# One core, hybrid MLA and mLSTM backbone: an early constant load, six banks for the output-gate tiles, a first chunk in stream tiles, and the values' products ahead of the convolution

## The chip, the cores and the metric

The kernel runs on one core of a Trainium2 chip. The metric is the device time of that core in microseconds (us), as the median of several runs; lower is better. Beside the runs there is one profiled execution with a trace of every instruction, and the profile is a view of that trace. PE is the matrix engine, PEld its weight loads, DVE, ACT and POOL the vector, scalar and general engines, SP the engine that issues the DMAs (SPq is its queue).

## The reference

Two layers run over 1024 latent tokens and 256 context tokens of width 1024. Layer 0 is multi-head latent attention. Layer 1, where the change lies, is a bidirectional mLSTM with 8 heads of 256 columns (16 blocks of 128, called features here). Cut to what matters:

```python
xm, z, og = jnp.split(h @ w_in, 3, axis=-1)
xc = jax.nn.silu(centred_dwconv(xm, conv_w, conv_b))      # 5 taps along the tokens
q, k, v = blockdiag(xc, w_q), blockdiag(xc, w_k), blockdiag(xm, w_v)
qkv = jnp.concatenate([q, k, v], axis=-1)
g = qkv @ w_if + b_if                                     # per direction: input and forget gate of 8 heads
li, lf = g[..., :8], jax.nn.log_sigmoid(g[..., 8:])
# per head and direction, chunk by chunk:
C_new = decay * C + einsum('bhl,bhld,bhle->bhde', a_end, vv, kk)   # running-max stabilised
hh    = num / maximum(abs(den), exp(-m))
y = ((rmsnorm(sigmoid(og) * h) * head_norm + skip * xc) * silu(z)) @ w_out
```

The kernel computes all of it in float32; each large product is three passes over a high and a low part (wh, wl for weights, hT..h, hT..l for tokens).

## The kernel before, in words

Layer 1 runs as stages, one after the other.

**Convolution stage** (phase_a, L911 to L1036). One turn of its loop per feature f. PE makes the columns xm of the *next* feature (tiles xps, by L78 to L80), the folded key-query matrix G and the gate columns gw of this one (pf, L980 to L982), the gate sums of all features in three banks (gps, L1011), the values (L1024, copied by ACT to vt at L1025 and stored to v_d) and the queries (qt, L1032). DVE does the four later taps (L995). At the end ACT copies the gate sums to graw (L1036).

**Gate scan** (gate_scan, L1210), a generator whose steps are taken inside the next stage. It loads a selection matrix sel and a bias (L1222, L1224), multiplies graw with sel (gsel, L1236), takes log-sigmoid and the running sums and maxima on DVE (gb, gM, gR), and turns the results by 40 PE transposes (gT, L1293) into column form (gcol, L1295). Tile gT has one bank, gsel two.

**Output-gate stage** (phase_z, L1093). For 8 heads, 2 halves of the contraction and 4 token tiles it runs 64 groups of 12 matmuls of 128x256 (po), in an order of PE and ACT that is written by hand. POOL splits the weights of w_og (wh, wl); ACT takes the sigmoid out of PSUM (og, L1136), SP stores it to og_d. Tiles po have five banks. The scan's steps stand before groups 0, 2, 32 and 37; before groups 39, 45, 51 and 57 the class Quarters prepares the next stage (L1080 on DVE, high parts t0h to t3h on ACT, low parts on DVE).

**Branch gate** (branch_gate, L1142): y products, PE without a pause.

**Recurrence** (phase_b, L1300). Chunks of 256 tokens. states() at L1357 loads x and v of a chunk from DRAM, transposes x on PE (S, L1369), splits the result (thh, thl) and forms the state updates pc and C. Before it, og0() issues the loads and splits of head 0's share of w_og for the remaining token tiles (L1047); the products of those tiles are dealt between the chunks by gate().

For engines other than PE and ACT in the output-gate stage, a scheduler sets the order from the order of the code. The lists of DMAs on SP and the lists of each engine run strictly in order. W.raw() and W.pair() hand out stream tiles from a small ring: a new load waits until the tile's earlier user is done.

Of the kernel before, what the change touches and what calls it, by code (L numbers as in the profile page):

```python
# [11 lines left out]
F32 = mybir.dt.float32  # L12
# [4 lines left out]
PSUM = bass.MemoryType.PSUM  # L17
# [895 lines left out]
def phase_a(nc, tc, ops, A, consts, mod, hT, S, W, graw, wx0, late):  # L913
# [3 lines left out]
    with ExitStack() as es:  # L917
# [49 lines left out]
        for f in range(NF):  # L967
# [21 lines left out]
                ops.split(g4[:, x, :, :8], g4[:, x, :, 8:16], pv, "act", "dve")  # L989
            xm = [sp.tile([P, CONV_W], F32R, name=f"xm{i}", bufs=1) for i in "hl"]  # L990
            ops.split(xm[0], xm[1], xp[:, 2 : 2 + CONV_W], "pool", "dve")
            xc = sp.tile([P, CONV_W], F32, name="xc")
            nc.scalar.activation(xc, xp[:, :CONV_W], AF.Identity, scale=cw[:, f, 0:1], bias=cw[:, f, 5:6])  # L993
            for j in range(1, 5):
# [13 lines left out]
            for b, (c0, n) in enumerate(cols):  # L1008
                for x, op in ((1, xm), (0, xh)):
                    for i in range(2):  # L1010
# [4 lines left out]
                            start=f == 0 and x == 1 and i == 0,  # L1015
                            stop=f == NF - 1 and x == 0 and i == 1,
                        )

            vt = sp.tile([P, NT, P], F32, name="vt")
            for t0, n in ((0, 2), (2, 4), (6, 4)):  # L1020
                ps = pm.tile([P, 4, P], F32, name="m")
                for i in range(n):
                    c0 = (t0 + i) * P + (4 if t0 else 2)
                    nc.tensor.matmul(ps[:, i], xp[:, c0 : c0 + P], bv, start=True, stop=True)  # L1024
                nc.scalar.copy(vt[:, t0 : t0 + n], ps[:, :n])  # L1025
            nc.sync.dma_start(S["v"][:, f * P : (f + 1) * P].rearrange("(c p) d -> p c d", p=P), vt)

            qt = qp.tile([P, SEQ], F32, name="qt")
            for j in range(2):
# [66 lines left out]
def phase_z(nc, tc, ops, A, hT, S, W, tiles, scan, e1, es):  # L1096
# [3 lines left out]
        tc.tile_pool(name=name, bufs=bufs, reuse_waits="tile", side="right", **kw)  # L1100
    )
    with ExitStack() as ez:
        sp, pp = right(ez, "z_s", 4), right(ez, "z_p", 5, space=PSUM)

        steps = {0, 2, 32, 37}
        later = (39, 45, 51, 57)
# [104 lines left out]
def gate_scan(nc, tc, ops, A, consts, S, keep, raw, es):  # L1211
# [6 lines left out]
    dec = keep.tile([P, 2, MH, NCH], F32, name="decay")  # L1218
    pl = lambda name, bufs=1, **kw: es.enter_context(tc.tile_pool(name=name, bufs=bufs, reuse_waits="tile", **kw))
    sp, pp = pl("g_s"), pl("g_p", 1, space=PSUM)  # L1220
    sel = sp.tile([P, 2, GR], F32, name="sel")
    nc.sync.dma_start(sel, A["gate_sel"])  # L1222
    bias = sp.tile([GR, 2], F32, name="gbias")
    nc.sync.dma_start(bias, A["b_if"])  # L1224
    keep01 = sp.tile([GR, T], F32, name="keep01")
    nc.sync.dma_start(keep01, A["chunk_keep"])
    yield
# [58 lines left out]
    yield  # L1286
    for c0 in range(0, NT, 3):
        n = min(3, NT - c0)
        pt = pp.tile([P, 3, 4, GR], F32, name="gT")
        for i in range(n):  # L1290
            for q in range(4):
                src = R[:, q] if q < 3 else gg
                nc.tensor.transpose(pt[:, i, q], src[:, (c0 + i) * P : (c0 + i + 1) * P], consts["idn"][:GR, :GR])  # L1293
        for d, r in enumerate(rows):
            nc.vector.tensor_copy(cols[d][:, c0 : c0 + n], pt[:, :n, :, r.start : r.start + MH])  # L1295
# [4 lines left out]
def phase_b(nc, tc, ops, A, consts, S, W, cols, dec, hT, es_h, es_w):  # L1300
# [3 lines left out]
    with ExitStack() as es, ExitStack() as ew, ExitStack() as eo:  # L1304
# [51 lines left out]
        def states(h, step, st):  # L1356

            for c in news[step]:
                hd = slice(h * 256, (h + 1) * 256)
                x = st["x"][c] = xp.tile([P, 2, U], F32, name="x", bufs=8)  # L1360
                nc.sync.dma_start(x, S["xcT"][2 * h : 2 * h + 2, :, c * U : (c + 1) * U].rearrange("k p t -> p k t"))
                v = st["v"][c] = vp.tile([P, 2, VW], F32, name="v", bufs=7)
                nc.sync.dma_start(v[:, :, :256], S["v"][c * U : (c + 1) * U, hd].rearrange("(a p) d -> p a d", p=P))
                nc.gpsimd.memset(v[:, :, 256:257], 1.0)
                nc.gpsimd.memset(v[:, :, 257:258], 0.0)
                pt = pw.tile([P, 2, 2, P], F32, name="S")
                for a in range(2):
                    for k in range(2):
                        nc.tensor.transpose(pt[:, a, k], x[:, k, a * P : (a + 1) * P], consts["idn"])  # L1369
                th = st["th"][c] = [sp.tile([P, 2, 256], F32R, name=f"th{i}", bufs=THB) for i in "hl"]  # L1370
                ops.split(th[0], th[1], pt.rearrange("p a k f -> p a (k f)"), "act", "dve")
            for i in (2 * step, 2 * step + 1):
                for d in range(2):
                    update(h, d, i, st)

            for d in range(2):
                if step == 1:
                    update(h, d, NCH - 2, st)
                if step == 3:
                    t, nxt = ORDERS[d][-2:]  # L1380
                    decay(h, d, t, st, st["C", d, nxt][0])
# [104 lines left out]
        new = lambda: {"x": {}, "v": {}, "th": {}}  # L1486
        ogs = lambda h: output_gate(nc, ops, A, S, hT, (W, po), h, range(NZ, 8))
        og0, *ogt = ogs(0)
        og0()
        o = W.raw().rearrange("p (t n) -> p t n", t=8 - NZ)  # L1490
        sts = [new() for _ in range(MH)]
        for step in range(NU - 1):
            states(0, step, sts[0])
            gate(0, ogt[step], o)
        units = [(h, c, sts[h]) for h in range(MH) for c in range(1, NU)]
        front(*units[0])
# [137 lines left out]
def build(nc, tc, A, out, dbg=None):  # L1634
    ops = Ops(nc)
    with ExitStack() as es:
# [30 lines left out]
        with ExitStack() as el:  # L1667
# [15 lines left out]
                el2.close()  # L1683

            gr = el.enter_context(tc.tile_pool(name="graw", bufs=1))
            graw = gr.tile([P, T], F32, name="graw")
            phase_a(nc, tc, ops, A, consts, mod, hT, S, W, graw, wx0, late)
            with ExitStack() as e1:
                scan = gate_scan(nc, tc, ops, A, consts, S, gk, graw, e1)
                next(scan)  # L1690
                with ExitStack() as et:
                    (cols, dec), Q = phase_z(nc, tc, ops, A, hT, S, W, range(NZ), scan, e1, et)
                    branch_gate(nc, tc, ops, A, S, W, Q)
# [106 lines left out]
```

## Time and profile before

| what | value |
|---|---|
| median of 3 runs | 2325.61 us (2319.2, 2325.61, 2329.93) |
| profiled execution | 2333.05 us |
| span of its trace, mean granted PE clock | 2331.3 us, 0.983 |
| PE, DVE, ACT, POOL busy | 95%, 72%, 53%, 51% |
| convolution stage, most of it | 1180 to 1410 us, PE busy 228.94 of 230 |
| its end and the output-gate stage | 1409 to 1527 us |
| branch gate to recurrence | 1655 to 1700 us, PE busy 36.87 of 45 |

PE is busy 95% of the span, so what it still loses lies in few places. A share over the whole span hides them; they are found by the waits of PE in a stretch, by the chain of waits, and by a table of stretches with the granted clock.

### The profile page before, as it was taken

The numbers are of one execution on the slowest core, as the hardware profiler recorded it, in microseconds if no ns is written. First come the engines' busy times: TensorE is split into PE (matmuls) and PEld (weight loads), VectorE is DVE, ScalarE is ACT, GpSimd is POOL, SyncE is SP. The second block draws the span as 40 slices with busy tenths as digits, with TensorE's granted clock in tenths as the row PEclk, the third lists the DMA queues.
The fourth block names the chain that finished last, engine by engine and source line by source line (L and its number), as shares of the span: only waits on it lengthen the run. The fifth ranks groups of instructions, "written<-read, shape, count | busy, mean of one in ns | idle before, by whom it ended". The sixth has DMA issues, their size and how long they took to land.

```text
span 2331.3 us, 38227 instructions
## 1 busy us (share of the span) xinstructions
PE 2216.7 (95%) x13404; PEld 1945.4 (83%) x13404; DVE 1670.8 (72%) x2871; ACT 1235.7 (53%) x2937; POOL 1186.6 (51%) x1586
## 2 busy tenths in 40 slices
PE   8999999999999999998999999899899999998998
PEld 4877798998998988887888887888788888896787
DVE  5588598999998988457765556554398888888321
ACT  4612487787887877332333333343466766676211
POOL 3324356565655645463332235622457778878321
PEclk9999999999999999999999999999999999999999
DMA  7066522222311211643444433423635555545531
GB/s 263 28 213 221 153 71 79 69 63 68 89 45 59 82 54 45 198 152 125 136 165 136 136 111 97 133 101 109 203 108 157 164 163 165 165 140 168 181 127 54
DMA packets 191579, 291.11 MB, mean 125 GB/s; under 512 B 14392, under 2 KB 134968, under 8 KB 191132
## 3 DMA queue, kind: packets, MB, share of 16 engines
q1 hardware_dynamic: 190860, 286.84, 39.3%
q8 instruction: 106, 1.74, 0.3%
q0 software_dynamic: 528, 1.84, 0.2%
q14 instruction: 85, 0.70, 0.1%
HBM read 198.00 MB, written 90.62 MB: 124 GB/s over the span
## 4 chain that ended last, share of the span: by engine, by line
PE 62%; DVE 14%; POOL 8%; DMA 7%; issue 5%; ACT 4%; SPq 1%; DVEq 0%; POOLq 0%; ACTq 0%
PE po L716 6%; PE y L1163 5%; PE tps L705 5%; PE yps L79 3%; PE yps L80 3%; PE yps L78 3%; PE S L78 3%; PE xps L79 3%; PE xps L80 3%; PE S L80 3%; PE xps L78 3%; PE S L79 3%; PE po L1427 2%; DVE modacc L204 2%; PE gps L1011 1%
## 5 line engine op out<-in xcount | busy, mean ns | idle before, releaser
L688 POOL TENSOR_SCALAR P<-P,sc 128x512 f32<-128x512 f32 (+1 forms) x384 | 244.4, 656 | 139.0 <-ACT P L644 64.7
L67 DVE TENSOR_TENSOR PTl<-tps,PTh 128x512 fp32r<-128x512 f32 x336 | 228.6, 682 | 12.2 <-ACT PTh L59 8.6
L705 PE MATMUL tps<-idn,P 128*128 128x128 f32 x1344 | 204.3, 275 | 10.0 <-POOL P L688 3.8
L59 ACT CAST PTh<-tps 128x512 fp32r<-128x512 f32 x336 | 196.2, 585 | 21.7 <-PE tps L705 20.2
L644 ACT ACTIVATE P<-S,nm 128x512 f32<-128x512 f32 x256 | 177.5, 694 | 50.3 <-DVE nm L643 47.3
L643 DVE TENSOR_REDUCE nm<-S 128x1 f32<-128x512 f32 x256 | 174.8, 683 | 17.4 <-PE S L80 13.8
L705 PEld LDWEIGHTS tps<-idn,P 128*128 128x128 f32 x1344 | 158.2, 142 | 15.9 <-issue 5.0
L1427 PE MATMUL po<-C,q 128*128 128x258 f32 x512 | 140.4, 393 | 7.1 <-ACT num L1423 6.0
L67 POOL TENSOR_TENSOR wl<-raw,wh 128x512 fp32r<-128x512 f32 x78 | 115.2, 1491 | 60.6 <-ACT wh L59 60.3
L716 PEld LDWEIGHTS po<-PTh,V 128*128 128x128 f32 x672 | 121.2, 191 | 27.7 <-ACT o L725 5.7
L716 PE MATMUL po<-PTl,V 128*128 128x256 f32 x672 | 137.1, 285 | 5.3 <-DVE PTl L67 5.3
L63 POOL TENSOR_SCALAR wh<-raw 128x512 fp32r<-128x512 f32 (+1 forms) x82 | 71.0, 878 | 137.4 <-PE xps L79 76.0
L716 PE MATMUL po<-PTh,V 128*128 128x256 f32 x672 | 138.4, 287 | 2.6 <-ACT o L725 2.3
L67 DVE TENSOR_TENSOR wl<-raw,wh 128x512 fp32r<-128x512 f32 (+2 forms) x65 | 75.0, 1164 | 68.1 <-POOL wh L63 50.3
L995 DVE SCALAR_TENSOR_TENSOR xc<-xp,cw,xc 128x1282 f32<-128x1282 f32 x64 | 110.9, 1734 | 13.2 <-ACT xc L993 11.7
L716 PEld LDWEIGHTS po<-PTl,V 128*128 128x128 f32 x672 | 105.6, 191 | 6.7 <-DVE PTl L67 6.5
L1333 DVE SCALAR_TENSOR_TENSOR ahl<-v,gcol,ahh 128x258 fp32r<-128x258 f32 x144 | 96.6, 674 | 13.6 <-ACT ahh L1332 13.2
L78 PE MATMUL pc<-ahh,thh 128*128 128x258 f32 x288 | 99.3, 346 | 6.7 <-DVE C L1350 3.4
L1427 PEld LDWEIGHTS po<-C,q 128*128 128x128 f32 x512 | 89.9, 196 | 17.7 <-ACT num L1423 8.1
L1350 DVE SCALAR_TENSOR_TENSOR C<-C,decay,pc 128x258 f32<-128x258 f32 x224 | 101.4, 472 | 1.4 <-PE pc L80 1.4
L730 POOL TENSOR_TENSOR gate<-o,gate 64x256 f32<-64x256 f32 x80 | 58.8, 738 | 74.2 <-DVE o L729 64.6
L78 PE MATMUL xps<-hT10h,wh 128*128 128x512 f32 (+1 forms) x272 | 94.6, 348 | 0.0
(732 smaller groups left out, 7758.4 us busy)
## 6 DMA issues: line engine op xcount, KB each, us to landing
raw<-in_w_og SPq DMA_DIRECT2D x32, 512.0 KB
qT<-q_d SPq DMA_DIRECT2D x16, 960.0 KB
adaw<-in_ada_w SPq DMA_DIRECT2D x48, 256.0 KB
q_d<-qs SPq DMA_DIRECT2D x24, 512.0 KB
xt<-in_xcat SPq DMA_DIRECT2D x20, 512.0 KB
v_d<-vt SPq DMA_DIRECT2D x16, 640.0 KB
x<-xcT_d SPq DMA_DIRECT2D x40, 256.0 KB
v<-v_d SPq DMA_DIRECT2D x40, 256.0 KB
```

The lines of the kernel that those rows point to most:

```text
L59: self.nc.scalar.copy(out, x)
L67: e.tensor_tensor(out, x, hi.bitcast(F32), ALU.subtract)
L78: mm(out, lh, rh, start=start, stop=False)
L79: mm(out, lh, rl, start=False, stop=False)
L80: mm(out, ll, rh, start=False, stop=stop)
L643: nc.vector.tensor_reduce(nm, S, axis=AX.X, op=ALU.max, negate=True)
L644: nc.scalar.activation(p, S, AF.Exp, bias=nm, accum_out=sm)
L688: nc.gpsimd.tensor_scalar(p, p, sc[:, a, j : j + 1], 1.0, ALU.mult, ALU.mult)
L705: nc.tensor.transpose(pt[:, kk * 256 + a * P : kk * 256 + (a + 1) * P], src, consts["idn"])
L716: nc.tensor.matmul(po, Vs[h][:, k].rearrange("p a d -> p (a d)"), PT[i][:, kk * 256 : kk * 256 + 256], start=k == 0 and i == 0, stop=k == ...
L1163: nc.tensor.matmul(ps, x, y, start=start, stop=stop, skip_group_check=more)
L1427: nc.tensor.matmul(pi[:, :VW], qa, C[:, k], start=k == 0, stop=k == 1)
```

## The change

Four edits, none of which changes the number of instructions on PE.

1. The loads of sel and gbias are issued before the convolution stage, into the pool of graw, and handed to gate_scan.
2. Tiles po get six banks. The transposes of gate_scan write to the two gsel banks; gT's own bank goes.
3. The first chunk of the recurrence (head 0, chunk 0) keeps x and v in stream tiles; og0() follows states(0, 0) instead of preceding it.
4. In each feature the values' products, their copies and the store to v_d stand ahead of the convolution, not behind the gate sums.

```diff
@@ phase_a, in the loop over f @@
             ops.split(xm[0], xm[1], xp[:, 2 : 2 + CONV_W], "pool", "dve")
+            vt = sp.tile([P, NT, P], F32, name="vt")
+            for t0, n in ((0, 2), (2, 4), (6, 4)):
...
+                nc.scalar.copy(vt[:, t0 : t0 + n], ps[:, :n])
+            nc.sync.dma_start(S["v"][:, f * P : (f + 1) * P].rearrange("(c p) d -> p c d", p=P), vt)
             xc = sp.tile([P, CONV_W], F32, name="xc")
...
-            vt = sp.tile([P, NT, P], F32, name="vt")
...
@@ phase_z @@
-        sp, pp = right(ez, "z_s", 4), right(ez, "z_p", 5, space=PSUM)
+        sp, pp = right(ez, "z_s", 4), right(ez, "z_p", 6, space=PSUM)
@@ gate_scan @@
-    sel = sp.tile([P, 2, GR], F32, name="sel")
-    nc.sync.dma_start(sel, A["gate_sel"])
-    bias = sp.tile([GR, 2], F32, name="gbias")
-    nc.sync.dma_start(bias, A["b_if"])
+    raw, sel, bias = raw
...
-        pt = pp.tile([P, 3, 4, GR], F32, name="gT")
+        pt = pp.tile([P, 512], F32, name="gsel", bufs=2)[:, : 12 * GR].rearrange("p (c q r) -> p c q r", q=4, r=GR)
@@ phase_b, states() and its caller @@
-                x = st["x"][c] = xp.tile([P, 2, U], F32, name="x", bufs=8)
+                early = h == 0 and c == 0
+                x = st["x"][c] = W.raw()[:, : 2 * U].rearrange("p (k t) -> p k t", k=2) if early else xp.tile([P, 2, U], F32, name="x", bufs=8)
...
-                v = st["v"][c] = vp.tile([P, 2, VW], F32, name="v", bufs=7)
+                v = st["v"][c] = W.raw()[:, : 2 * VW].rearrange("p (a d) -> p a d", a=2) if early else vp.tile([P, 2, VW], F32, name="v", bufs=7)
...
-        og0()
-        o = W.raw().rearrange("p (t n) -> p t n", t=8 - NZ)
         for step in range(NU - 1):
             states(0, step, sts[0])
+            if step == 0:
+                og0()
+                o = W.raw().rearrange("p (t n) -> p t n", t=8 - NZ)
@@ the caller @@
-            graw = gr.tile([P, T], F32, name="graw")
+            graw, sel, gbias = (gr.tile(s, F32, name=n) for s, n in (([P, T], "graw"), ([P, 2, GR], "sel"), ([GR, 2], "gbias")))
+            nc.sync.dma_start(sel, A["gate_sel"])
+            nc.sync.dma_start(gbias, A["b_if"])
             phase_a(nc, tc, ops, A, consts, mod, hT, S, W, graw, wx0, late)
```

Three places where instructions move. The first is SP's queue from the end of the convolution stage through the first output-gate tiles, in the kernel before:

```order
L1026 DMA v_d<-vt 128x10x128
L1034 DMA qT_d<-qt 128x1024
L1222 DMA sel<-in_gate_sel 128x80
L1224 DMA gbias<-in_b_if 40x2
L1226 DMA keep_16215<-in_chunk_keep 40x1280
L1137 DMA og_d<-og 128x256 x2
L1114 DMA raw<-in_w_og 128x1024
L1137 DMA og_d<-og 128x256 x2
L1274 DMA negM_d<-gR 8x1280 x2
L1114 DMA raw<-in_w_og 128x1024
```

The same stretch of SP's queue in the changed kernel:

```order
L1000 DMA v_d<-vt 128x10x128
L1114 DMA raw<-in_w_og 128x1024
L1223 DMA keep_16215<-in_chunk_keep 40x1280
L1034 DMA qT_d<-qt 128x1024
L1137 DMA og_d<-og 128x256 x2
L1114 DMA raw<-in_w_og 128x1024
L1137 DMA og_d<-og 128x256 x2
L1114 DMA raw<-in_w_og 128x1024
L1271 DMA negM_d<-gR 8x1280 x2
L1137 DMA og_d<-og 128x256 x2
```

The load of sel has left the end of the stage (it stands some 120 entries earlier), keep comes ahead of the last store of queries, and one more load of w_og stands ahead of the stores of negM, which wait for the scan.

The second place is DVE in one turn of the convolution loop. Before (xml and xcl are low parts, xc the taps, Gl and gw the low parts of what pf gave):

```order
L67 TENSOR_TENSOR xml<-xp_13369,xmh 128x1282
L995 SCALAR_TENSOR_TENSOR xc<-xp_13369,cw,xc 128x1282 x3
L67 TENSOR_TENSOR xcl<-xc,xch 128x1282
L985 SCALAR_TENSOR_TENSOR Gl<-m,Gh 128x128
L67 TENSOR_TENSOR gw_13367<-m,gw_13367 128x4x8 x2
```

The same turn in the changed kernel:

```order
L1004 SCALAR_TENSOR_TENSOR xc<-xp_13373,cw,xc 128x1282
L985 SCALAR_TENSOR_TENSOR Gl<-m,Gh 128x128
L1004 SCALAR_TENSOR_TENSOR xc<-xp_13373,cw,xc 128x1282
L67 TENSOR_TENSOR gw_13371<-m,gw_13371 128x4x8
L1004 SCALAR_TENSOR_TENSOR xc<-xp_13373,cw,xc 128x1282
L67 TENSOR_TENSOR gw_13371<-m,gw_13371 128x4x8
L67 TENSOR_TENSOR xcl<-xc,xch 128x1282
```

Gl and the two gw now stand between the taps and ahead of xcl.

The third place is SP's queue ahead of the recurrence. Before, both loads of head 0's w_og have gone out earlier, and x and v of the first chunks follow the gate's stores (sz_d), the broadcasts nM and the loads of og:

```order
L1398 DMA nM<-negM_d 128x256 x4
L1435 DMA og<-og_d 128x2x256 x2
L1167 DMA sz_d<-u_18375 128x512
L1361 DMA x<-xcT_d 128x2x256
L1363 DMA v<-v_d 128x2x256
L1361 DMA x<-xcT_d 128x2x256
```

In the changed kernel:

```order
L1360 DMA raw<-xcT_d 128x2x256
L1167 DMA sz_d<-u_18192 128x512
L1167 DMA sz_d<-u_18240 128x512
L1167 DMA sz_d<-c_18278 128x512
L1167 DMA sz_d<-u_18220 128x512
L1362 DMA raw<-v_d 128x2x256
L1047 DMA raw<-in_w_og 128x1024
L1309 DMA mask<-in_mask 128x256
L1311 DMA hns<-in_hn_skip 128x32
L1167 DMA sz_d<-u_18327 128x512
L1397 DMA nM<-negM_d 128x256 x4
L1434 DMA og<-og_d 128x2x256
L1047 DMA raw<-in_w_og 128x1024
```

The first chunk's x and v (tiles raw now) have moved to where the two loads of w_og were, and these two to behind them, the second one close to where the first chunk's x stood.

## Rows read from the trace of the kernel before

**Rows 1.** Stretches: busy time and count per engine, granted PE clock, DMA share, GB/s.
```profile
1180.00:1410.00 230.00, 228.94 (x1288) 198.95 (x1286) 129.51 (x111) 85.58 (x150) 73.07 (x65) 1.00 0.41 137
...
1480.00:1540.00 60.00, 55.63 (x385) 52.60 (x385) 41.49 (x49) 18.02 (x38) 27.64 (x21) 0.93 0.27 85
...
1655.00:1700.00 45.00, 36.87 (x248) 34.14 (x247) 19.72 (x38) 22.90 (x45) 23.16 (x52) 0.92 0.73 230
```

**Rows 2.** Waits of PE, 1405 to 1545 us: total us, times, longest.
```profile
PE gsel L1236 <- DMA sel<-in_gate_sel: 5.1, 1, 5.1
PE po L78 <- ACT og L1136: 4.8, 3, 2.7
PE gT L1293 <- DVE gcol L1295: 1.8, 3, 0.6
```

**Rows 3.** Chain that ended last, 1400 to 1540 us: start, us, what.
```profile
1410.33 3.62 DMA sel<-in_gate_sel
...
1450.48 1.22 DVE gR L1272
...
1452.88 5.00 DMA og_d<-og
...
1486.65 0.62 ACT t0h L59
```

**Rows 4.** PE in order of time, at the convolution stage's end.
```profile
1408.55 0.39 PE L80 MATMUL m<-xch,Gl 128*128 128x512 f32 x1
1414.00 3.76 PE L1236 MATMUL gsel<-graw,sel 128*40 128x512 f32 x6 [5.06 <-DMA sel<-in_gate_sel]
...
1420.48 0.38 PE L78 MATMUL po<-wh,hT10h 128*128 128x256 f32 x1
```

**Rows 5.** PE, 1456 to 1518 us: bank waits, transposes, and matmuls at either clock.
```profile
1458.42 0.39 PE L78 MATMUL po<-wh,hT10h 128*128 128x256 f32 x1 [1.68 <-ACT og L1136]
...
1478.95 0.51 PE L1293 MATMUL gT<-idn,gR 40*128 40x40 f32 x3 [0.60 <-DVE gcol L1295]
...
1481.95 0.41 PE L79 MATMUL po<-wl,hT10h 128*128 128x256 f32 x1
1482.16 0.41 PE L80 MATMUL po<-wh,hT10l 128*128 128x256 f32 x1
...
1487.08 0.28 PE L80 MATMUL po<-wh,hT10l 128*128 128x256 f32 x1
...
1487.32 0.28 PE L79 MATMUL po<-wl,hT10h 128*128 128x256 f32 x1
...
1515.54 0.39 PE L78 MATMUL po<-wh,hT10h 128*128 128x256 f32 x1 [2.71 <-ACT og L1136]
```

**Rows 6.** POOL in the output-gate stage and ahead of the recurrence.
```profile
1445.31 4.53 POOL L67 TENSOR_TENSOR wl<-raw,wh 128x512 fp32r<-128x512 f32 x2
...
1655.27 2.54 POOL L67 TENSOR_TENSOR wl<-raw,wh 128x512 fp32r<-128x512 f32 x2
```

**Rows 7.** PE at the start of the recurrence.
```profile
1661.72 0.39 PE L1163 MATMUL y<-hT11h,wl 128*128 128x512 f32 x1
1667.94 1.09 PE L1369 MATMUL S<-idn,x 128*128 128x128 f32 x4 [5.84 <-DMA x<-xcT_d]
...
1672.46 0.41 PE L80 MATMUL po<-wh,hT11l 128*128 128x256 f32 x1
```

**Rows 8.** Chain that ended last, 1640 to 1690 us.
```profile
1659.70 8.11 DMA x<-xcT_d
```

**Rows 9.** One turn of the convolution loop, ACT.
```profile
1262.04 0.59 ACT L945 COPY xp<-xps 128x512 f32<-128x512 f32 x1 [4.33 <-PE xps L80]
...
1282.53 0.59 ACT L945 COPY xp<-xps 128x512 f32<-128x512 f32 x1 [4.33 <-PE xps L80]
```

**Rows 10.** The same turn, DVE.
```profile
1264.20 2.43 DVE L995 SCALAR_TENSOR_TENSOR xc<-xp,cw,xc 128x1282 f32<-128x1282 f32 x1
...
1267.96 4.72 DVE L995 SCALAR_TENSOR_TENSOR xc<-xp,cw,xc 128x1282 f32<-128x1282 f32 x3
```

More of the change, by code (lines that the diff above doesn't have):

```diff
@@ L991, in phase_a @@
             ops.split(xm[0], xm[1], xp[:, 2 : 2 + CONV_W], "pool", "dve")
+            vt = sp.tile([P, NT, P], F32, name="vt")
+            for t0, n in ((0, 2), (2, 4), (6, 4)):
+                ps = pm.tile([P, 4, P], F32, name="m")
+                for i in range(n):
+                    c0 = (t0 + i) * P + (4 if t0 else 2)
+                    nc.tensor.matmul(ps[:, i], xp[:, c0 : c0 + P], bv, start=True, stop=True)
+                nc.scalar.copy(vt[:, t0 : t0 + n], ps[:, :n])
+            nc.sync.dma_start(S["v"][:, f * P : (f + 1) * P].rearrange("(c p) d -> p c d", p=P), vt)
             xc = sp.tile([P, CONV_W], F32, name="xc")
@@ L1017, in phase_a @@
                         )
-            vt = sp.tile([P, NT, P], F32, name="vt")
[L1020 to L1026, printed above, removed]
             qt = qp.tile([P, SEQ], F32, name="qt")
@@ L1685, in build @@
             gr = el.enter_context(tc.tile_pool(name="graw", bufs=1))
-            graw = gr.tile([P, T], F32, name="graw")
+            graw, sel, gbias = (gr.tile(s, F32, name=n) for s, n in (([P, T], "graw"), ([P, 2, GR], "sel"), ([GR, 2], "gbias")))
+            nc.sync.dma_start(sel, A["gate_sel"])
+            nc.sync.dma_start(gbias, A["b_if"])
             phase_a(nc, tc, ops, A, consts, mod, hT, S, W, graw, wx0, late)
             with ExitStack() as e1:
-                scan = gate_scan(nc, tc, ops, A, consts, S, gk, graw, e1)
+                scan = gate_scan(nc, tc, ops, A, consts, S, gk, (graw, sel, gbias), e1)
                 next(scan)
```

## The prediction

> **What bounds the kernel now.** I read the span first, as the table above has it: of the 2333.05 us of the profiled execution all but 1.75 lies in it. Then the table of stretches, to see where PE, busy 95% overall, is not: the convolution stage leaves it 1.1 us in 230, but the stretch 1480 to 1540 leaves 4.4 us at a clock of 0.93, and 1655 to 1700 8.1 us at 0.92 [rows 1]. Third, the waits of PE around the output-gate stage: 5.1 us for sel, 4.8 in three waits for a bank of po, 1.8 in three for the bank of gT [rows 2]. Last the chain of waits, which says that these waits do decide the end: it runs through the load of sel, the scan down to gR, a store of og, and later the cast t0h on ACT [rows 3]. So the stage that matters is the output-gate stage, then the start of the recurrence.
>
> **Edit 1, selection matrix.** The last query matmul starts at 1408.55 and ends by about 1408.9; gsel starts at 1414.00 after 5.06 us idle [rows 4], 3.62 of it the load [rows 3]. When sel is there already, gsel needs only graw, which ACT copies before those last matmuls end. I take 5.0. After that idle gsel ran at 1.2 GHz, 6.48 us from its start to the first po [rows 4]; without the idle it should keep 2.4 GHz. ACT's copies pace it about as much, so I take 0.5 of what a full halving of its first 3.76 us would give (1.9); bounds 0 and 1.9. The scan depends on gsel and comes 5.5 us earlier with it, so its chain keeps its place beside PE. The new loads stand ahead of the gate and convolution weights on SP, while PE still has the first feature's columns to make: cost 0, and without that cover at most the 3.62 us of such a load.
>
> **Edit 2, six banks.** A group of 12 matmuls of 256 columns takes 1.44 us at full clock (one matmul each 0.12 us, two of them in the 0.24 from 1487.08 to 1487.32 [rows 5]; 64 groups would be 92 us of the 107 from 1420.48 to the next stage). A sixth bank lets PE run one group further, so each wait for a bank shrinks by at most 1.44.
>
> The Trainium skill (Perfetto Trace Analysis, Matmul Optimizations) advises to use all eight PSUM banks, as the change does; taken at its word all 4.8 us of these waits would go. The rows say that each wait ends when a late ACT comes round [rows 2, 5], which a bank only postpones, so the sum goes by groups.
>
> The wait at 1458.42 is 1.68 [rows 5]: it falls to about 0.24, gain 1.44 (bounds 0 and 1.68). It hangs on a store of og issued at 1452.88 and taking 5.00 behind the negM stores, which wait for gR at 1450.48 [rows 3]; gR and PE both move by 5.5, so the wait is otherwise the same.
>
> The transposes write 12, 12, 12 and 4 into one bank and wait 0.60 each time for two copies to gcol [rows 2, 5]. With two banks round three waits only for the copies of round one, which run beside round two. About 0.4 of 1.8 remains: gain 1.4 (bounds 0.8 and 1.8).
>
> In the third round the transposes already run at half clock (0.51 for three) and the po matmuls behind them too, 0.41 instead of 0.28 as shown, 0.21 apart instead of 0.12 [rows 5]. That costs 16 matmuls at 0.09, and 0.9 for the last transposes: 2.4 us. What PE did before the fall was 24 small transposes with one 0.6 pause between. Without the pauses they end before the point at which it fell, or just behind; I cannot decide that and take half, 1.2 (bounds 0 and 2.4).
>
> The Trainium skill (TensorE: Matmul & The Clock Gate, Part 4: PE-mode transpose) says that transposes do not count as busy in the way matmuls do. By that the clock falls with or without pauses, and this term would be 0, the sum 1.2 less. The row shows a fall in the midst of transposes, which fits it without proving it.
>
> Then the end of the stage. From t0h at 1486.65 on, ACT holds the casts of Quarters among the sigmoids, and DVE, busy 41.5 us of 60 here [rows 1], makes their sums and low parts. PE waits 2.71 us, to 1515.54, for a sigmoid behind these casts [rows 3, 5]. That train of casts starts when ACT has evacuated the groups behind the transposes, so it moves with PE at that place. It does not become shorter. The sixth bank buys one group before PE must wait, and then the wait is there again and so is the slow clock behind it (16 matmuls at 0.09, about 1.5): gain 1.44 (bounds 0 and 2.71 + 1.5 = 4.2).
>
> Output-gate stage together: 5.0 + 0.5 + 1.44 + 1.4 + 1.2 + 1.44 = 11.0. The branch gate behind it starts that much earlier and is full of PE work, so nothing is given back there.
>
> **Edit 3, start of the recurrence.** The last y matmul starts at 1661.72; S waits 5.84 for x and starts at 1667.94, and PE then runs at 1.2 GHz to about 1672.7 [rows 7]. x was issued at 1659.70 and took 8.11 [rows 8]. Now x and v of this chunk go out where the w_og loads went, over 10 us earlier, and S starts at about 1662.1. Late next is the second w_og load: its stream tile is that of the first, whose split on POOL ended at 1657.8 [rows 6], so it goes out at 1658, behind the same backlog. Landing as x did, 8 to 9 us later, it is there at 1666 to 1667, and POOL's first wh half (0.6) lets PE go on at about 1667.85. Until then PE has done the transposes and 12 po matmuls, 1.9 us of work that took 3.65 at half clock before. So 3.65 us of old work is off the path; the clock falls again in the new pause of about 3.9 us, and as many microseconds of other work now run at half rate as before, which takes 1.8 back. Net 1.8; the first chunk's casts now stand behind two og copies on ACT instead of one, 0.4 each, so I take 1.5 (bounds 0, the load as late as 1669.7, and 5.8, no pause at all).
>
> **Edit 4, values ahead.** The same matmuls in another order in a stage where PE is full: 0 by itself. It puts Gl and gw between the taps on DVE. A turn is 20.49 us [rows 9]. Counted by columns, 0.69 of it stands between the end of xps and the third values' tile, which needs the bank that the second gw frees: PE is there 14.2 us into the turn. DVE by its rows: the last three taps end at 1272.68, 10.6 into the turn [rows 10], and the small ones between them add some 0.7: 11.3. So 2.9 us are spare, and PE waits for nothing. Bounds: 0 above; below, see the third rival.
>
> **Sum.** 11.0 + 1.5 = 12.5. Against the profiled execution 2333.05 - 12.5 = 2320.5; the median of the runs is 7.4 us lower than that execution, and the same subtraction gives 2325.6 - 12.5 = 2313.1, say 2313. About 0.5%, 11.6 us or 2314.0, is what a measurement can tell from no change; the forecast lies just on the fast side of it.
>
> **Rivals.**
> Everything goes: the two clock dips and all bank waits. 5.06 + 1.9 + 1.68 + 1.8 + 2.4 + 4.2 + 1.5 = 18.5, 2307. For it: clock falls have always come behind a pause here. Against it: the train of casts, bound by DVE, sets the end of the stage.
>
> Only the selection matrix pays: POOL becomes the bound. Under the scan its splits slow down; the pair at 1445.31 takes 4.53 [rows 6], twice that of 1655.27, and ends at 1449.84, when PE has just reached that block. What PE gains by banks it would then lose waiting for wl. 5.0 + 0.5 and little else: 2320. Against it: among the waits of PE before there is none for wl [rows 2].
>
> Slower: the interleaved Gl and gw hold up DVE, and the third values' tile waits. It decides from 2.9 us late; each further microsecond costs 16 turns, so 5 us late costs 2.1 x 16 = 34, less 12.5: 2347. For it: the first tap took 2.43 once and 1.57 at other times [rows 10], and DVE has other work in the first turns. Against it: four taps at 2.43 make only 3.5 us.
>
> **Numbers.** The forecast has 0.52, and I put 0.32 of it below 2314.0 and 0.20 above; everything goes 0.15 (faster); selection only 0.25 (same); slower mechanism 0.08, of which 0.02 is a small version that ends within 0.5%. Faster 0.47, same 0.47, slower 0.06. The range 2303 to 2326 holds the first three cases and leaves out the slower one.
>
> **What would show it.** Edit 1: no idle ahead of gsel, gR 5 to 6 us earlier relative to the start of the branch gate's loads. Edit 2: no wait of gT on gcol above 0.3; a first bank wait below 0.5; a last bank wait still there, about 2 us. If the last wait is gone, the train of casts was not the bound. Edit 3: S right behind y, then a pause of 3 to 5 us that ends with wh. Edit 4: gps every 20.5 us. The forecast is wrong if gps comes at more than 20.6, if PE waits for wl between 1430 and 1470, or if the pause at the recurrence is longer than 5.84.

## The result, and the profile after

The changed kernel took 2313.49 us in the median of six runs (2307.95 to 2314.12), the kernel before 2324.24 in six runs of the same set: ratio 0.995 [0.9935, 0.9966]. A second set gave 2311.51 against 2324.58, ratio 0.9938 [0.9926, 0.995]. So it is faster by 0.5 to 0.6%, 10.7 and 13.1 us; 2313 was forecast.

The two profiled executions lie further apart, and that must be cleared away first: 2333.05 before and 2307.95 after, 25.1 us. Only 14.3 us of it stand in the stretches around the change. Another 3.4 stand in code that both kernels share: layer 0 up to the first convolution matmul took 1042.85 us before and 1039.49 after, and in the other traces of this study, with the same instructions there, 1035.9 to 1042.9. And 6.9 stand in the recurrence from its first to its last state product, of which edit 3 touches the start alone: 425.67 before and 418.77 after, but 422.70 and 422.02 when both kernels were traced once more. So the traces are compared by stretches from landmark to landmark, two executions of each kernel (times of the first instruction of each kind on PE, in us):

| stretch | before | before again | after | after again | change of the means | forecast |
|---|---|---|---|---|---|---|
| first xps to last query matmul | 365.70 | 365.37 | 364.17 | 364.60 | -1.1 | 0 |
| to the first po | 11.93 | 11.87 | 5.39 | 5.38 | -6.5 | -5.5 |
| to the first transpose | 55.40 | 55.10 | 54.91 | 54.91 | -0.3 | -1.4 |
| to the next po | 5.69 | 5.67 | 2.62 | 2.61 | -3.1 | with the next row: |
| to the first y | 45.63 | 45.74 | 41.14 | 44.11 | -3.1 | -4.0 |
| to the last y | 134.52 | 134.53 | 137.41 | 137.41 | **+2.9** | 0 |
| to the first pc | 17.84 | 17.84 | 16.74 | 14.37 | -2.3 | -1.5 |
| all of these | 636.70 | 636.11 | 622.39 | 623.39 | -13.5 | -12.5 |

The sum agrees, its terms less so: the output-gate stage gained 13.0 instead of 11.0, the convolution 1.1 instead of nothing and the start of the recurrence 2.3 instead of 1.5, while the branch gate, where nothing was expected, took 2.9 back.

The waits of PE in the changed kernel from 1395 to 1545 us (total us, times, longest), in place of [rows 2]:

```profile
PE po L78 <- ACT og L1136: 2.6, 2, 1.9
PE y L1163 <- ACT u L1184: 0.7, 1, 0.7
PE gsel L1233 <- ACT gf L1234: 0.2, 1, 0.2
PE po L79 <- POOL wl L67: 0.2, 1, 0.2
```

The wait for sel (5.1) and the three for gcol (1.8) are gone. Of the waits for a bank of po, 2.6 of 4.8 remain, and there is a first one for wl, 0.2. Where they stand is seen in PE's instructions in order of time, the changed kernel (start, us, what, idle before and its releaser); they answer to [rows 4, 5]:

```profile
1403.66 0.39 PE L80 MATMUL m<-xch,Gl 128*128 128x512 f32 x1
1403.98 2.51 PE L1233 MATMUL gsel<-graw,sel 128*40 128x512 f32 x6
1406.66 2.45 PE L1233 MATMUL gsel<-graw,sel 128*40 128x512 f32 x6 [0.17 <-ACT gf L1234]
1409.05 0.38 PE L78 MATMUL po<-wh,hT10h 128*128 128x256 f32 x1
...
1444.93 0.39 PE L79 MATMUL po<-wl,hT10h 128*128 128x256 f32 x1 [0.17 <-POOL wl L67]
...
1447.94 0.38 PE L78 MATMUL po<-wh,hT10h 128*128 128x256 f32 x1 [0.71 <-ACT og L1136]
...
1463.96 0.37 PE L1290 MATMUL gsel<-idn,gR 40*128 40x40 f32 x3
...
1466.57 0.38 PE L78 MATMUL po<-wh,hT10h 128*128 128x256 f32 x1
...
1498.98 0.39 PE L78 MATMUL po<-wh,hT10h 128*128 128x256 f32 x1 [1.91 <-ACT og L1136]
...
1645.13 0.40 PE L1163 MATMUL y<-hT11h,wl 128*128 128x512 f32 x1
1645.36 0.60 PE L1368 MATMUL S<-idn,raw 128*128 128x128 f32 x4
...
1651.46 0.50 PE L78 MATMUL po<-wh,hT11h 128*128 128x256 f32 x2 [4.07 <-POOL wh L63]
```

The selection products follow the last query product without idle time, and the 40 transposes run from 1463.96 to 1466.57 without a wait between them. S follows the last y at once [rows 7], and the pause that remains, 4.07, ends with wh, whose load is the late one, as POOL's line shows:

```profile
1650.79 1.20 POOL L63 TENSOR_SCALAR wh<-raw 128x512 fp32r<-128x512 f32 x2 [3.19 <-DMA raw<-in_w_og]
```

That load went out on SP at 1641.20, 4.2 us before the end of y, and the split of it began 9.6 us later; x took 8.11 before [rows 8].

What took time back is seen in two windows over all of y, first of the kernel before and then of the changed one (length, busy time and count of PE, PEld, DVE, ACT, POOL, granted clock, DMA share, GB/s):

```profile
1527.20:1661.95 134.75, 133.92 (x590) 110.06 (x588) 62.95 (x81) 48.10 (x83) 43.78 (x45) 1.00 0.32 107
```

```profile
1507.71:1645.36 137.65, 136.86 (x590) 110.22 (x589) 63.46 (x82) 47.87 (x83) 42.49 (x43) 1.00 0.32 106
```

The same 590 matmuls, the same idle time (0.83 and 0.79), the clock full in both: the matmuls themselves are longer. A view of tile y says which (count, then duration in ns: least, median, most). Before:

```profile
L1163 PE MATMUL y<-t0h,wh x28: 389/389/389, 1534.1 to 1655.8; 128*128 128x512 f32 x28
```

After:

```profile
L1163 PE MATMUL y<-t0h,wh x28: 392/396/399, 1514.6 to 1639.1; 128*128 128x512 f32 x28
L1163 PE MATMUL y<-hT10h,wh x56: 387/389/496, 1507.7 to 1636.5; 128*128 128x512 f32 x56
```

Products that stream the tiles of Quarters (t0h to t3l) went from 389 to between 392 and 399; of those that stream hT, hT10l with wh went from 389 to 393 and the others have the median they had. The starts tell it more plainly (means, waits left out): behind a t tile the next matmul begins some 234 ns later, behind an hT tile 227 to 230, before the change 226 to 227 behind either. The t tiles make up 2.4 us of the 2.9, the hT tiles 0.5.

### The profile page after: what moved, and what is told of

It is laid out like the page before. It is cut to its first block, busy times and chain, and to the rows that moved or that the text cites. A ratio compares the mean times of both kernels' runs of the same rounds, so it can differ in the third digit from the quotient of the medians.

```text
span 2306.2 us, 38206 instructions
## 1 busy us (share of the span) xinstructions
PE 2206.0 (96%) x13404; PEld 1933.5 (84%) x13404; DVE 1669.1 (72%) x2871; ACT 1235.9 (54%) x2937; POOL 1189.8 (52%) x1586
## 4 chain that ended last, share of the span: by engine, by line
PE 62%; DVE 13%; POOL 9%; DMA 6%; issue 6%; ACT 4%; SPq 1%; DVEq 0%; POOLq 0%; ACTq 0%
PE y L1163 6%; PE po L716 5%; PE tps L705 5%; PE yps L79 3%; PE yps L80 3%; PE yps L78 3%; PE xps L78 3%; PE xps L80 3%; PE xps L79 3%; PE S L78 3%; PE S L80 3%; PE S L79 3%; PE po L1426 2%; PE m L998 2%; PE gps L1020 1%
## 5 line engine op out<-in xcount | busy, mean ns | idle before, releaser
L80 PE MATMUL xps<-hT10h,wl 128*128 128x512 f32 (+1 forms) x272 | 93.9, 345 | 0.7 <-DVE wl L67 0.7
```

The source lines that it names most:

```text
L80: mm(out, ll, rh, start=False, stop=stop)
```

## The experiments

There are twelve runs in four groups, three of them of kernels that had run before. First each edit alone, then the address behind the 2.9 us, then the transposes, and last ACT's order at the end of the output-gate stage.

### Each edit alone

**e1_sel** is the kernel before with edit 1 only:

```diff
-    sel = sp.tile([P, 2, GR], F32, name="sel")
-    nc.sync.dma_start(sel, A["gate_sel"])
...
+    raw, sel, bias = raw
@@ the caller @@
+            graw, sel, gbias = (gr.tile(s, F32, name=n) for s, n in (([P, T], "graw"), ([P, 2, GR], "sel"), ([GR, 2], "gbias")))
+            nc.sync.dma_start(sel, A["gate_sel"])
```

> The kernel before with edit 1 alone (sel and gbias loaded ahead of the convolution stage). Theory A, each edit pays in its own place: no idle before gsel (5.06 gone), gsel to the first po 5.1 us instead of 6.5, the three bank waits and the gT waits unchanged; 6 to 7 us faster, ratio about 0.997. Theory B, the gain is a chain in which the scan decides: the stores of negM still hold SP, so 5 us or less. Theory P, the slower y matmuls of the branch gate in the changed kernel (231 ns apart instead of 227) come from the tiles that this edit moves by 352 bytes: y takes 137 us here instead of 134 and the net is only 3 to 4 us.

Measured: 2322.11, ratio 0.9996 [0.9985, 1.0006]. The waits of PE in this kernel, 1395 to 1520 us:

```profile
PE po L78 <- ACT og L1136: 5.3, 3, 2.7
PE gT L1290 <- DVE gcol L1292: 1.8, 3, 0.6
PE gsel L1233 <- ACT gf L1234: 1.3, 1, 1.3
PE y L1163 <- ACT u L1184: 0.7, 1, 0.7
PE po L79 <- POOL wl L67: 0.2, 1, 0.2
```

The wait for sel is gone. With sel there, four of the selection products stand ahead of the last six query matmuls, so this kernel has another order on PE than the changed one; a wait of gsel for ACT's copy (1.3) comes behind them. From the first xps to the first po it takes 370.95 us instead of 377.4, so 6.5 are gained. The first bank wait grows to 2.18, the clock is at its lower level for most of the four microseconds behind it (0.57 of full), and the stretch from po to the transposes is 57.89 instead of 55.25, which takes back 2.6. And y takes 137.40: the 2.9 us come with this edit and no other. From the first xps to the first pc it gains 3.6 (632.80), 1.7 of it at the start of the recurrence (16.10 for 17.84), which this edit does not touch. The runs show no difference from before.

**e2_banks** is edit 2 alone:

```diff
-        sp, pp = right(ez, "z_s", 4), right(ez, "z_p", 5, space=PSUM)
+        sp, pp = right(ez, "z_s", 4), right(ez, "z_p", 6, space=PSUM)
...
-        pt = pp.tile([P, 3, 4, GR], F32, name="gT")
+        pt = pp.tile([P, 512], F32, name="gsel", bufs=2)[:, : 12 * GR].rearrange("p (c q r) -> p c q r", q=4, r=GR)
```

> The kernel before with edit 2 alone (six banks for po, the transposes write to the gsel banks). Theory A: the idle before gsel stays 5.06, the wait of po at the first bank wait falls from 1.7 to below 0.4, no wait of gT above 0.3, no fall of the clock behind the transposes, a last bank wait of about 2 us; first po to first y 99 us instead of 107, so 6 to 8 us faster, ratio 0.997. Rival B, the casts of Quarters on ACT and DVE set the end of the stage: 2 to 3 us faster, first po to first y 104. Rival C, POOL's splits become the bound: waits for wl, under 2 us faster.

Measured: 2317.43, ratio 0.9974 [0.9964, 0.9983]; first xps to first pc 627.18, 9.2 less than before; first po to first y 99.1. It is the largest single edit. Its waits, 1395 to 1520 us:

```profile
PE gsel L1236 <- DMA sel<-in_gate_sel: 5.0, 1, 5.0
PE po L78 <- ACT og L1136: 1.9, 1, 1.9
...
```

The first bank wait is gone altogether here, while 0.71 of it is there in the changed kernel. The difference comes with edit 1, and DVE shows how. In the kernel before and in e2_banks, Quarters' first sums (b, L1080) are done while DVE has nothing else, since gsel waits for sel; in the changed kernel, as in e1_sel, some of them stand ahead of the scans and one behind the first two. DVE before:

```profile
1419.42 0.69 DVE L1080 TENSOR_TENSOR b<-b,b 128x512 f32<-128x512 f32 x1
...
1427.87 6.15 DVE L1257 TENSOR_TENSOR_SCAN gb<-keep,gf 32x1280 f32<-32x1280 f32 x2
1434.06 2.34 DVE L1258 COPY gbl<-gb 32x10 f32<-32x10 f32 x2
```

DVE in the changed kernel:

```profile
1418.07 6.31 DVE L1254 TENSOR_TENSOR_SCAN gb<-keep,gf 32x1280 f32<-32x1280 f32 x2
1424.41 1.61 DVE L1080 TENSOR_TENSOR b<-b,b 128x512 f32<-128x512 f32 x1
...
1441.84 1.88 DVE L1269 TENSOR_SCALAR gR<-gM 40x1280 f32<-40x1280 f32 x1
```

gR starts 37.9 us behind the first gsel (1403.98), against 36.5 before (1414.00 to 1450.48, [rows 3, 4]). The selection products themselves take 1.4 us less, so counted from the first po gR starts 2.8 us later: 32.8 behind it instead of 30.0. The store of og behind the negM stores is issued 35.4 behind the first po instead of 32.4. ACT, which waits for it, goes on 3.0 us after the issue instead of 5.1, so its next sigmoid comes 1.0 later (38.5 for 37.5). PE gets there 1.9 later, with the sixth bank and a short wait for wl, and that leaves 0.7 of the 1.7. The sigmoid behind that store, before and in the changed kernel:

```profile
1457.98 0.66 ACT L1136 ACTIVATE og<-po 128x256 f32<-128x256 f32 x2 [13.73 <-DMA og_d<-og]
```

```profile
1447.50 0.66 ACT L1136 ACTIVATE og<-po 128x256 f32<-128x256 f32 x2 [14.63 <-DMA og_d<-og]
```

**e3_chunk** is edit 3 alone:

```diff
+                early = h == 0 and c == 0
-                x = st["x"][c] = xp.tile([P, 2, U], F32, name="x", bufs=8)
+                x = st["x"][c] = W.raw()[:, : 2 * U].rearrange("p (k t) -> p k t", k=2) if early else xp.tile([P, 2, U], F32, name="x", bufs=8)
...
-        og0()
+            if step == 0:
+                og0()
```

> The kernel before with edit 3 alone (first chunk's x and v in stream tiles, the loads of head 0's w_og behind them). Theory A: S follows the last y at once, a pause of about 4 us for wh follows, the first pc comes 17 us after the last y instead of 18; 1 to 2 us faster. Rival D, the edit also orders the later loads (q and x) better: the waits of S for q fall from 7.8 to about 3 us and the recurrence to the end gets 5 us shorter, 6 us faster in all. Rival E: nothing within 2 us, the recurrence's own chain absorbs it.

Measured: 2321.79, ratio 0.9985 [0.9974, 0.9996]; last y to first pc 16.61 instead of 17.84, so 1.2 us, near the 1.5 of the forecast. All other stretches are those of before. But this stretch varies without the edit too: e1_sel took 16.10, e2_banks 16.37 and e4_values 16.56, at a granted clock of 0.89 or 0.90 in it, against 0.79 in e3_chunk and 0.81 before. At like clocks the edit shows less: near 0.8 two traces with it have 16.61 and 17.06 and three without it 17.71 to 17.84; near 0.9 five with it have 15.54 to 16.74, mean 15.99, and three without it a mean of 16.34. At one clock edit 3 is thus worth 0.3 to 1.0 us; the rest goes with the clock, and the runs do not tell whether the edit moves that.

**e4_values** is edit 4 alone:

```diff
+            vt = sp.tile([P, NT, P], F32, name="vt")
+            for t0, n in ((0, 2), (2, 4), (6, 4)):
...
             xc = sp.tile([P, CONV_W], F32, name="xc")
...
-            vt = sp.tile([P, NT, P], F32, name="vt")
-            for t0, n in ((0, 2), (2, 4), (6, 4)):
```

> The kernel before with edit 4 alone (values' products ahead of the convolution in each feature). Theory A: PE is full in this stage, its order changes nothing, 0 to 2 us faster (the two small waits of gps for xcl and gw, 0.9 us, go). Rival: the turn gets longer than 20.49 us because Gl and gw stand between the taps on DVE, slower by 16 times the excess.

Measured: 2323.02, ratio 0.9993 [0.9982, 1.0004]. From the first xps to the first pc it gains 5.5 (630.93): 1.9 ahead of the first po, 1.4 in the convolution and 1.3 at the start of the recurrence, which both lie within the spread of the other kernels, 1.1 from the first po to the transposes, where the first bank wait is 0.41 instead of 1.68 and 1.38, and 0.4 in the transposes, less 0.6 ahead of y. The 1.9 are the load: with the values gone from the end of the stage, the load of sel is issued sooner, and PE is idle 3.20 us ahead of gsel where it was 5.06:

```profile
1409.64 2.75 PE L1237 MATMUL gsel<-graw,sel 128*40 128x512 f32 x3 [3.20 <-issue]
```

So edits 1 and 4 remove part of the same wait. By the stretches the four edits alone give 3.6 + 9.2 + 1.0 + 5.5 = 19.3, together 13.5. By the medians they give 2.0 + 6.7 + 2.3 + 1.1 = 12.1, together 10.7 and 13.1, so the time of the whole kernel does not show the overlap.

### The 2.9 us of the branch gate

In the kernel before, sel and gbias lie with the scan's tiles; edit 1 puts them behind graw. Worked out from the tile sizes, sel takes 320 bytes of each partition and gbias 8, taken here as rounded up to 32, which no trace shows: what is laid out behind them, the t tiles among it, then moves by 352 bytes. If the address is the cause, a wider gbias undoes it. **pad512** and **pad384** are the changed kernel with gbias widened, so that the shift is 512 or 384 bytes; the second one has 48 replaced by 16:

```diff
-... (([P, T], "graw"), ([P, 2, GR], "sel"), ([GR, 2], "gbias")))
+... (([P, T], "graw"), ([P, 2, GR], "sel"), ([GR, 48], "gbias")))
-            nc.sync.dma_start(gbias, A["b_if"])
+            nc.sync.dma_start(gbias[:, :2], A["b_if"])
```

> The changed kernel with gbias made 192 bytes wide, so that the pool of graw moves what follows it by 512 bytes and not by 352. Theory P (the place of the tiles t0h to t3l, the operands streamed by the y matmuls, decides how far apart those matmuls start): y takes 134.5 us instead of 137.4 and y matmuls are 227 ns apart on all operands; 2.9 us faster than the changed kernel, median about 2310.5. Rival (the y matmuls slow down because other engines are elsewhere in their work): y stays at 137.4 and the median at 2313.5.

> The same with 64 bytes for gbias: a move by 384 bytes, so the address of t0h leaves the remainder 32 by 64 (as before the change) but another remainder by 128, 256 and 512 than at 512 bytes. If the remainder by 64 decides: 134.5 us for y; if a coarser one decides: 137 us or something between.

Measured: pad512 2312.21, ratio 0.9939 [0.9926, 0.9952]; pad384 2313.38 in one run. In pad512 y takes 134.53 us as before, in pad384 136.95. The window over y in pad512:

```profile
1511.33:1646.09 134.76, 133.93 (x590) 110.22 (x589) 63.16 (x81) 48.07 (x83) 41.81 (x43) 1.00 0.33 107
```

Tile y in pad512:

```profile
L1163 PE MATMUL y<-t0h,wh x28: 388/390/390, 1518.2 to 1640.0; 128*128 128x512 f32 x28
```

And of pad384:

```profile
L1163 PE MATMUL y<-t0h,wh x28: 392/398/399, 1520.3 to 1644.4; 128*128 128x512 f32 x28
```

Nothing differs between these kernels but where tiles lie, so the place of the tiles is shown to be the cause. Which tile's place it is, is not shown: all that lies behind graw moves together, and the products that stream hT, which lies ahead of graw and did not move, slowed down a little too. 384 bytes, a multiple of 128, does not restore the speed and 512 does; whether 256 would was not tried, and why the place matters stays open. In the time of the whole kernel the 2.9 us are not told from the spread: 2312.21 beside 2313.49 and 2311.51 without the pad.

### The transposes and the clock behind them

**share** is the kernel before with the transposes in the banks of gsel and still five banks for po:

```diff
-        pt = pp.tile([P, 3, 4, GR], F32, name="gT")
+        pt = pp.tile([P, 512], F32, name="gsel", bufs=2)[:, : 12 * GR].rearrange("p (c q r) -> p c q r", q=4, r=GR)
```

> The kernel before with only the transposes written to the gsel banks, po still at five banks. Theory A: the transposes take 2.6 us instead of 5.7 and the clock stays at 2.4 GHz behind them, the bank waits stay (1.7 and 2.7 us or more). So this half gives about 5 us of the 7.4 that edit 2 gave between the first po and the first y, and the sixth bank the rest. Rival (the fall of the clock comes from the transposes themselves): 2 us for the waits, the clock falls all the same.

Measured: 2316.79 in one run. The 40 transposes take 2.62 us to the next po, as in the changed kernel, so two banks alone do this; the waits for a bank of po are those of before:

```profile
PE po L78 <- ACT og L1136: 4.8, 3, 2.7
...
```

The clock behind the transposes was read in the four microseconds that follow them. In the five traces with gT's own bank, and so with pauses, it falls each time. Without pauses it falls in six of nine: in share, pad512, pad384, pad_later, later_only and after_again, and not in the profiled run of the changed kernel, in e2_banks and in pad_later_again. Two windows of after_again, behind the transposes and behind the last bank wait:

```profile
1467.97:1471.97 4.00, 4.00 (x24) 4.00 (x24) 0.45 (x4) 0.39 (x1) 0.32 (x1) 0.63 0.75 256
1503.97:1507.97 4.00, 4.00 (x25) 4.00 (x25) 3.97 (x7) 2.90 (x6) 0.00 (x0) 0.68 0.59 176
```

The same two windows of the profiled run of the changed kernel:

```profile
1466.57:1470.57 4.00, 4.00 (x35) 4.00 (x34) 0.48 (x4) 1.16 (x3) 0.33 (x1) 1.00 0.85 262
1498.98:1502.98 4.00, 4.00 (x33) 4.00 (x34) 3.96 (x8) 1.53 (x5) 0.00 (x0) 1.00 0.30 90
```

PE is busy without a gap in all four; in after_again the clock is at the lower level for most of the first two, and 24 and 25 matmuls run where 35 and 33 do. Each fall costs about 1.5 us, which is why the stretch to the first y took 41.14 in the one execution and 44.11 in the other. So pauses between transposes are not needed for the fall. The Trainium skill (TensorE: Matmul & The Clock Gate, Part 4: PE-mode transpose) says that transposes do not count as activity as matmuls do. Six of these nine traces agree with it, three don't show the fall; what decides between them stays open.

### The end of the output-gate stage

The forecast held that the casts of Quarters set the end of this stage, whatever banks there are. ACT in the changed kernel, in order of time:

```profile
1485.50 0.93 ACT L1136 ACTIVATE og<-po 128x256 f32<-128x256 f32 x3
1494.41 0.62 ACT L59 CAST t0h<-t 128x512 fp32r<-128x512 f32 x1 [7.99 <-DVE t L1080]
...
1498.02 0.62 ACT L59 CAST t3h<-b 128x512 fp32r<-128x512 f32 x1 [0.67 <-DVE b L1080]
1498.55 1.20 ACT L1136 ACTIVATE og<-po 128x256 f32<-128x256 f32 x4
```

ACT stands idle for 7.99 us at a cast whose sums DVE has not finished, with four sigmoids queued behind it that PE waits for. It is the order of ACT's list that does this, and one number moves it. **pad_later** is pad512 with the third step of Quarters five groups later, so that four sigmoids stand ahead of its casts:

```diff
-        later = (39, 45, 51, 57)
+        later = (39, 45, 56, 57)
```

> pad512 with the third step of Quarters before group 56 instead of 51, so that the sigmoids of groups 52 to 55 stand ahead of its casts on ACT. Theory A (the train of casts and their DVE work sets the end of the output-gate stage): the last bank wait of 1.9 us goes, but the train ends as much later, and the branch gate's first y or its first weights wait instead: within 1 us of pad512. Rival (the order on ACT alone causes that wait): 1.9 us faster than pad512.

Measured: 2303.94 (2303.36 to 2306.12), ratio 0.9909 [0.9894, 0.9924]. PE's waits from 1400 to 1530 us:

```profile
PE po L78 <- ACT og L1136: 0.7, 1, 0.7
PE y L1163 <- ACT u L1184: 0.7, 1, 0.7
PE y L1163 <- ACT wh L59: 0.3, 1, 0.3
...
```

The last bank wait is gone, and y, which uses those casts, pays 0.6 us (135.11 for 134.53). Three more runs go with it: the changed kernel again, the changed kernel with this number alone (**later_only**), and pad_later again, with the kernel before beside them.

> The changed kernel once more, for a second trace. Its first profiled execution was the fastest of its runs and had no fall of the clock in the output-gate stage. If such falls come and go between executions of one kernel, this trace has one behind the transposes or behind the last bank wait, 44 us from the transposes to the first y instead of 41; if they are tied to the build, 41 again. Theory P: y takes 137.4 us here too, whatever the clock does.

> The changed kernel with only the third step of Quarters moved from before group 51 to before group 56, t tiles at the slower place. The move's own share: the last bank wait of 1.9 us and the fall of the clock behind it go, 3.5 us faster than the changed kernel by the output-gate stage alone; y stays at 137.4. If most of the 8 us that separated pad_later from pad512 belongs to the move, 6 to 8 us faster.

> The kernel before once more, for a second trace: 11.9 us from the last query matmul to the first po, 55.4 from there to the transposes, 5.7 for these, 45.6 to the first y, 134.5 for y, as in the first. What differs from the first trace outside that stage (the attention layer, the recurrence) is the spread of one kernel between executions: 3 us or more in each.

> pad512 with the third step of Quarters before group 56, once more, beside the changed kernel on the same chip. If 2303.9 us was no accident of that set of runs: 2303 to 2306, 8 to 10 us below the changed kernel; theory from the traces alone, that is 2.9 us for the place of the t tiles and 3.5 for the last wait: 6 us below it.

Measured: after_again 2311.51, ratio 0.9938 [0.9926, 0.995]; later_only 2308.96, 0.9932 [0.992, 0.9944]; pad_later_again 2305.23, 0.9921 [0.9906, 0.9937]; before_again one run, 2330.01. ACT in later_only:

```profile
1492.51 0.39 ACT L1136 ACTIVATE og<-po 128x256 f32<-128x256 f32 x1 [3.53 <-issue]
1493.95 0.39 ACT L1136 ACTIVATE og<-po 128x256 f32<-128x256 f32 x1 [1.05 <-PE po L80]
...
1497.11 0.61 ACT L59 CAST t0h<-t 128x512 fp32r<-128x512 f32 x1
```

Now each sigmoid follows its products, and the cast finds its sums ready. The stretch to the first y is 40.46 with one fall of the clock, for 44.11 with two in after_again and 41.14 with none in the first trace of the changed kernel; without a fall pad_later_again has 38.97. The median of later_only is 2.6 below that of after_again, less than the 3.5 that were expected, and the intervals of the two ratios overlap: alone, in this set, the number is not told from no change. Both steps together bring 6.3 us in this set (2311.51 to 2305.23; these intervals overlap as well), and the traces account for most of that: from first xps to first pc the two traces of either kernel have a mean of 617.8, against 622.9. In the first set pad_later and pad512 lie apart in every run (2303.36 to 2306.12 against 2307.86 to 2315.96). Of that larger gain (2312.21 to 2303.94, by `later` alone) the stretches explain 2.8; the rest lies in code that is the same. pad_later is the best version of all that ran, 19 to 22 us faster than the kernel before in the two sets.

## Why the prediction was right, and where its terms were not

The time came out as forecast, and for the greater part by the steps that were named. That the sum came so near is luck in part: some 3.9 us more than forecast were gained in the other stretches, and 2.9 were lost in the branch gate.

- **Edit 1, idle ahead of gsel** (5.0): right, 5.06 to 0 [rows 4].
- **Edit 1, clock of gsel** (0.5): mis-sized. From gsel to the first po it is 5.07 instead of 6.48, 1.4 us. Two groups of six matmuls take 2.51 and 2.45 with 0.17 of wait for ACT between them, so ACT's copies paced the stretch less than was assumed.
- **Edit 2, first bank wait** (1.44): failed. The wait fell from 1.68 and 1.38 to 0.71 and 0.70, so the sign "a first bank wait below 0.5" did not come, and the stretch is only 0.3 shorter, since a new wait for wl takes some 0.4 of it back. The sentence that failed is that gR and PE "both move by 5.5, so the wait is otherwise the same": gR comes 2.8 us later counted from the first po, because gsel got shorter on PE and DVE's sums of Quarters, which the old idle time had covered, now stand among the scans. e2_banks shows that the bank itself removes the wait.
- **Edit 2, transposes** (1.4 of waits, and the slow last ones, 0.9, in a term taken by half): mis-sized, 3.1 came. No wait on gcol is left at all, and in none of the traces with two banks are the transposes themselves slow any more.
- **Edit 2, clock behind the transposes** (half of 2.4): taking half was about right, for another reason than the pauses. The fall behind them comes in six of nine traces. The rival in which everything goes rested on falls that come only behind a pause; share refutes that, with a fall and no pause between the transposes.
- **Edit 2, last bank wait** (1.44): 2.71 became 1.91, so 0.8, and the fall behind it came in one of the two traces, as dear as it was put (1.5). That the casts hold up the sigmoids was right; that their train sets the end of the stage was not. later_only and pad_later keep every cast and lose the wait. The Trainium skill (Perfetto Trace Analysis, Matmul Optimizations) advises all eight banks. The kernel before used eight too (five for po, two for gsel, one for gT), and in the changed kernel, with six and two, 2.6 of the 4.8 us of bank waits are still there: here it is not the number that decides.
- **"Nothing is given back there"** (branch gate): failed, +2.9 us. PE was full in this stretch, and from that I concluded that it could not become longer. e1_sel and pad512 show that the loss comes with the place of the tiles that edit 1 moves. A full engine can still take longer for each instruction.
- **Edit 3** (1.5): right in order and place, too large in size. S stands right behind y, the pause is 4.07 (3 to 5 forecast) and ends with wh. The stretch gained 1.1 and 3.5 in the two traces and 1.2 in e3_chunk, but at like clocks the edit is worth 0.3 to 1.0. The granted clock in the stretch, 0.90 and 1.00 in the two traces for 0.81 before, makes up the rest; the forecast had it fall again as before, and in after_again it did not fall.
- **Edit 4** (0): 1.1 us came in the convolution, but that stretch runs from 363.3 to 365.3 with the edit and from 364.1 to 365.7 without it (e1_sel aside, where selection products stand in it), so it isn't told from nothing. Its effect on the load of sel, which e4_values shows alone, was not foreseen; in the whole change edit 1 covers it.

The rivals: "only the selection matrix pays" fell, since e1_sel moves the time by nothing measurable and e2_banks, without that edit, by 6.7 us. Its sign did come by the letter: PE waits for wl at 1444.93, between 1430 and 1470, but for 0.17 us in one place. POOL has little left, though; from 1410 to 1466 it is busy for 50.84 of 56 us. The slower one fell as well: PE is busy for every microsecond of the convolution's bulk in the changed kernel and its turns are 20.52 us apart, so the third values' tile holds up nothing:

```profile
1180.00:1400.00 220.00, 220.00 (x1239) 191.78 (x1238) 123.58 (x110) 80.54 (x140) 66.03 (x60) 1.00 0.40 135
```

## What to carry to other kernels

When a wait is taken away, ask which work used the idle time on the *other* engines: it will now stand in the middle of the chain that moved forward. Where an engine waits for a bank, look at what stands ahead of the evacuation in the evacuating engine's list before adding a bank; here a sixth bank cut the last wait by 0.8 us, and one number in the order removed it. And before a single profile of each kernel is compared, compare the stretches that the change does not touch.

## What the runs showed of the hardware

- The place of tiles in their partitions changes the rate of matmuls: 234 ns instead of 227 from start to start for streamed tiles moved by some 352 bytes, 233 at 384, and 227 again at 512; 2.9 us in 590 matmuls. Matmuls whose streamed tile did not move took 227 to 230.
- The granted clock can fall, with PE busy throughout, behind 40 small transposes in 2.6 us, and the same program falls in one execution and not in the next.
- Times differ where nothing is changed. The six runs of the kernel before in the first set went from 2319.2 to 2329.93. Over all traces layer 0, with the same instructions, went from 1035.9 to 1042.9; the three kernels that were traced twice differ by at most 1.0 there and by 0.5 to 3.3 in the recurrence, so how much of the 7 us lies between executions and how much between kernels is open.
